# The fourth weight sum of a seven-product unit: an accumulating DMA from DRAM in the place of a VectorE instruction

## The chip, the cores and the metric

The kernel runs on one core of one Trainium2 chip. The metric is the device time of one execution in microseconds; three executions of the kernel before gave 2301.18, 2301.93 and 2302.52 us. TensorE, VectorE, ScalarE, GpSimd and SyncE are called PE, DVE, ACT, POOL and SP, as the profile calls them.

## The reference

Two decoder layers over 256 tokens of width 2048, all in float32. What concerns this change is the second half of a layer, the feed-forward part, and there only its matrix products with weights:

```python
h = rms_norm(x, ffn_norm[l])
x = x + (jax.nn.silu(h @ w_gate[l]) * (h @ w_up[l])) @ w_down[l]
```

`w_gate` and `w_up` are 2048 x 5632, `w_down` is 5632 x 2048, and the activations have 256 rows.

## The kernel before, in words

**Float32 by three products.** PE multiplies operands of a rounded float32 form. Each weight tile `raw` (128 partitions x 4 blocks x 512 columns, 1 MB) is split into two such tiles: ACT copies it to `wh`, which rounds it, and DVE subtracts, `wl = raw - wh`. The same is done to the activations, and `mm3` (line 836) issues three matmuls for each block: high x high, high x low, low x high. A product of four blocks is therefore twelve matmuls of 512 columns.

**Units.** In the feed-forward part the work is cut into units. A unit computes a 2 x 2 block of results (two halves of the tokens by two weight columns, for instance a block of `w_gate` and the same block of `w_up`) from a 2 x 2 block of weights. It uses a scheme with seven products in the place of eight, which needs sums of weight blocks and sums of activation blocks. The weight blocks are called b11, b12, b22 and b21. Sums are made in place by DVE with `w_sum`, one instruction for a whole tile. The activations' sums ("forms") are made once by `make_forms` and used by many units. A unit of `w_gate` and `w_up`, and most of `w_down`, has 4 blocks a product (`s` is 4); the last chunk's two `w_down` units of each layer have 2. There are 17 units in a layer, 34 in all. After its seven products a unit has plain products for the rest of its sum, which need no weight sums.

**The order of the seven.** The products run in the order p1, p5, p6, p2, p7, p3, p4. `early` makes e = b12 - b11 and b12 := b22 - b12 some items ahead. Then p1 splits b11 and makes b11 := b12 + b11; p5 splits e; p6 splits the new b11; p2 makes b11 := b21 - b11 (the sum that this change is about) and splits b21; p7 splits b12; p3 splits b22; p4 splits the last b11. The results are gathered in four PSUM banks, named C1, CX, CY and CZ in the trace (C, CX, CY, CZ where numbers are left out), so the products in this order write C, CZ, CX, C, CX, CY, CX: the fourth product, p2's, is the second run of C in a unit, and the seventh, p4's, is the CX run behind CY.

**What sets the order.** Every engine runs its instructions in the order in which the program lists them. A list of items is made; `prep` of an item (the splits and sums) is written out ahead of its `run` (the matmuls), as far ahead as six tile slots allow, which is three products of four blocks. A small model of the engines' queues (`Queues`, with costs in `act_cost` and `dve_cost`) decides at build time where other jobs (transposes, activation splits, residual sums) are written in between. All weight loads are issued by SP, line 796; a load waits until a slot among 22 is free.

Of the kernel before, what the change touches and what calls it, by code (L numbers as in the profile page):

```python
# [12 lines left out]
ALU = mybir.AluOpType  # L13
# [10 lines left out]
W = 512  # L24
# [8 lines left out]
KC = 4  # L33
HK = 2
S_GU = 4
FORMS = ("11", "22", "S1", "S3", "S2", "12", "S4")

SLOTS = 22
PLAIN_RAW, PLAIN_RING = 3, 4
# [102 lines left out]
def trunk_kernel(ctx: ExitStack, tc: tile.TileContext, aps: dict):  # L142
    nc = tc.nc
# [3 lines left out]
    dve = Engine(q, nc.vector, "dve", dve_cost)  # L147
# [16 lines left out]
    def slot(shape, dtype, name):  # L164

        return gen.tile(list(shape), dtype, tag="g", name=name)
# [55 lines left out]
    def add(steps, limit=BACKLOG_NS):  # L222
        jobs.append(Job(steps, limit))
        jobs.sort(key=lambda job: -job.limit)
# [7 lines left out]
    def drain(ready):  # L232
        stuck = 0
        while not ready():
            assert stuck < 2000, "operand is never made"
            stuck += 1
            q.pe += 100
            run_jobs(1000)
# [344 lines left out]
    class Forms:  # L583
# [5 lines left out]
        def at(self, f):  # L589
            h = self.halves[FORMS.index(f)]  # L590
            return h[:, 0, :self.s, :], h[:, 1, :self.s, :]
# [27 lines left out]
    def make_forms(F, xg):  # L619

        def quarter(t, h):
            return xg[:, h, :F.s, t * P:(t + 1) * P]
        a11, a12, a21, a22 = quarter(0, 0), quarter(0, 1), quarter(1, 0), quarter(1, 1)

        def split(f, src):
            hi, lo = F.at(f)
            act.activation(out=hi, in_=src, func=ACTF.Copy)
            dve.tensor_tensor(out=lo, in0=src, in1=hi.bitcast(F32), op=ALU.subtract)
            F.ready.add(f)
        split("11", a11)  # L630
        split("22", a22)
        dve.tensor_tensor(out=a22, in0=a21, in1=a22, op=ALU.add)
        dve.tensor_tensor(out=a21, in0=a11, in1=a21, op=ALU.subtract)
        yield
        split("S1", a22)
        split("12", a12)
        dve.tensor_tensor(out=a11, in0=a22, in1=a11, op=ALU.subtract)
        dve.tensor_tensor(out=a12, in0=a12, in1=a11, op=ALU.subtract)
        yield
        split("S2", a11)  # L640
        split("S3", a21)
        split("S4", a12)

# [50 lines left out]
    class Chunk:  # L694
# [32 lines left out]
        def form(self, f, k):  # L727
            drain(lambda: self.F is not None)
            return self.F.get(f, k)
# [61 lines left out]
    def dma_one(r):  # L791
        n = sum(src.shape[1] for src in r.srcs)
        r.tile = slot([P, n, W], F32, "raw")
        k = 0
        for src in r.srcs:
            nc.sync.dma_start(out=r.tile[:, k:k + src.shape[1], :], in_=src)
            k += src.shape[1]
        live[0] += 1
# [6 lines left out]
    def need(r):  # L805
        while r.tile is None:
            dma_one(raws[n_raw[0]])
            n_raw[0] += 1
        return r.tile

    def split_w(src, parts=1):

        n = src.shape[1]
        if 2 * n <= 4:
            both = slot([P, 2, n, W], F32R, "w")
            wh, wl = both[:, 0], both[:, 1]
        else:
            wh, wl = slot([P, n, W], F32R, "wh"), slot([P, n, W], F32R, "wl")
        saved, q.chain = q.chain, q.pe
        for k in range(parts):  # L820
            sl = slice(k * n // parts, (k + 1) * n // parts)
            act.activation(out=wh[:, sl, :], in_=src[:, sl, :], func=ACTF.Copy)
            dve.tensor_tensor(
                out=wl[:, sl, :], in0=src[:, sl, :], in1=wh[:, sl, :].bitcast(F32), op=ALU.subtract)
        q.chain = saved
        return wh, wl

    def w_sum(out, in0, in1, op):
        saved, q.chain = q.chain, q.pe
        dve.tensor_tensor(out=out, in0=in0, in1=in1, op=op)  # L830
        q.chain = saved

    def mm3(out, x, wh, wl, start, stop):
        hi, lo = x
        for n, (a, b) in enumerate(((hi, wh), (hi, wl), (lo, wh))):
            nc.tensor.matmul(  # L836
                out=out, lhsT=a, rhs=b, start=start and n == 0, stop=stop and n == 2,
                skip_group_check=True)
# [32 lines left out]
    def unit(s, quarter, plains, form, done, lead=1):  # L871

        bank = {}
        b11, b12, b22, b21 = (Raw([quarter(*kn)], UNIT_RAW) for kn in ((0, 0), (0, 1), (1, 1), (1, 0)))
        raws.extend((b11, b12, b22, b21))
        U = {}

        def new_bank(name):  # L880
            drain(lambda: mm_lease.free)
            mm_lease.free.pop(0)
            bank[name] = mm_p.tile([P, W], F32, tag="mm", name="C" + name)

        def copy(out, in_):
            saved, q.chain = q.chain, q.pe
            act.activation(out=out, in_=in_, func=ACTF.Copy)
            q.chain = saved

        def early():  # L890
            x11, x12, x22 = need(b11), need(b12), need(b22)
            U["e"] = slot([P, s, W], F32, "e")
            live[0] += 1
            w_sum(U["e"], x12, x11, ALU.subtract)
            w_sum(x12, x22, x12, ALU.subtract)

        def p1(it, parts=1):
            it.w = split_w(b11.tile)
            w_sum(b11.tile, b12.tile, b11.tile, ALU.add)

        def p5(it, parts=1):
            it.w = split_w(U["e"])
            live[0] -= 1

        def p6(it, parts=1):
            it.w = split_w(b11.tile)

        def p2(it, parts=1):
            w_sum(b11.tile, need(b21), b11.tile, ALU.subtract)
            it.w = split_w(b21.tile)  # L910
            live[0] -= 1

        def p7(it, parts=1):
            it.w = split_w(b12.tile)
            live[0] -= 1

        def p3(it, parts=1):
            it.w = split_w(b22.tile)
            live[0] -= 1

        def p4(it, parts=1):
            it.w = split_w(b11.tile)
            live[0] -= 1

        def product(it, f, name, start):
            wh, wl = it.w
            for k in range(s):
                x = form(f, k)
                mm3(bank[name], x, wh[:, k, :], wl[:, k, :], start and k == 0, k == s - 1)
                q.pe += 3 * MM_NS  # L930
                run_jobs()

        def r1(it):
            new_bank("1")
            product(it, "11", "1", True)
            new_bank("X")
            copy(bank["X"], bank["1"])

        def r5(it):
            new_bank("Z")  # L940
            product(it, "S1", "Z", True)
            U["s5"], U["s3"] = (tmp.tile([P, W], F32, tag="u", name=n) for n in ("s5", "s3"))
            copy(U["s5"], bank["Z"])

        def r6(it):
            product(it, "S2", "X", False)
            new_bank("Y")
            copy(bank["Y"], bank["X"])

        def r2(it):  # L950
            product(it, "12", "1", False)

        def r7(it):
            product(it, "S3", "X", False)
            copy(U["s3"], bank["X"])

        def r3(it):
            product(it, "S4", "Y", False)
            w_sum(bank["Z"], bank["Z"], U["s3"], ALU.add)

        def r4(it):
            product(it, "22", "X", False)
            w_sum(bank["Y"], bank["Y"], U["s5"], ALU.add)

        for p, r in ((p1, r1), (p5, r5), (p6, r6), (p2, r2), (p7, r7), (p3, r3), (p4, r4)):
            items.append(Item(1 if s <= 2 else 2, UNIT_RING, p, r))
        early_at[len(items) - 7 - lead] = early

        names = {(0, 0): "1", (1, 0): "Y", (0, 1): "X", (1, 1): "Z"}
        for i, (n, srcs, ops) in enumerate(plains):  # L970
            r = Raw(srcs, UNIT_RAW)
            raws.append(r)

            def prep(it, parts=1, r=r):
                it.w = split_w(need(r))
                live[0] -= 1

            def run(it, i=i, n=n, ops=ops):
                wh, wl = it.w
                for t in range(NT):  # L980
                    for k, op in enumerate(ops):
                        mm3(bank[names[n, t]], op(t), wh[:, k, :], wl[:, k, :], False, k == len(ops) - 1)
                        q.pe += 3 * MM_NS
                        run_jobs()
                    if i >= len(plains) - 2:
                        add(done(n, t, bank[names[n, t]]), FFN_LIMIT)
            items.append(Item(2, UNIT_RING, prep, run))
# [238 lines left out]
```

## Time and profile before

| | |
|---|---|
| three executions | 2301.18, 2301.93, 2302.52 us |
| median | 2301.93 us |
| the profiled execution | 2301.2 us |
| its span from the first to the last instruction | 2299.0 us |
| PE busy | 2261.3 us, 98% of the span |
| DVE busy | 1834.0 us, 80% |
| ACT busy | 1325.0 us, 58% |
| POOL busy | 52.4 us, 2% |
| granted clock of PE, mean | 0.999 of full speed |
| loads of weights | 438.69 MB on SP's queue, packets took 53.0% of 16 DMA engines' time |

The span is what the trace covers; 2.2 us of the execution's time lie around it. PE is busy nearly all of the time, so another engine matters only where PE stands and waits for it. The views that tell this are the groups of PE's instructions (their last columns give the idle time ahead of them and what ended it) and the timeline of one stretch, engine by engine.

### The profile page before, as it was taken

The page shows a single profiled execution, that of the slowest core. Times are in us where ns is not written, and L with a number is a line of the kernel's source. Part 1 is how long each engine was busy: PE and PEld are TensorE (multiplying, and loading weights), DVE is VectorE, ACT ScalarE, POOL GpSimd, SP SyncE. Part 2 cuts the span into 40 slices and gives each one's busy share as a digit, 9 for nine tenths or more (in the row PEclk, how much of TensorE's full clock was granted, in tenths as well). Part 3 has the DMA queues.
Part 4 walks back from the last instruction along what each step waited for, and adds up shares of the span by engine and source line. Part 5 has one row for each costly group of instructions (what it writes and reads, how often), then busy time and mean ns, then how long its engine had stood idle before and what let it go on. Part 6 is the DMA issues. An engine that isn't in the chain of part 4 may idle for free.

```text
span 2299.0 us, 25930 instructions
## 1 busy us (share of the span) xinstructions
PE 2261.3 (98%) x10249; PEld 1864.1 (81%) x10249; DVE 1834.0 (80%) x1721; ACT 1325.0 (58%) x1590; POOL 52.4 (2%) x36
## 2 busy tenths in 40 slices
PE   9999999999999999999999999999999999999999
PEld 7888888878788878888788888887787888788887
DVE  6666766889999898998765666768899998989986
ACT  6455565565664665656555555646656556556563
POOL 0100000000000000000000001000000000000000
PEclk9999999999999999999999999999999999999999
DMA  9554455454465644745545444554545556447453
GB/s 361 176 183 165 165 175 204 174 198 165 183 237 183 224 179 159 264 181 201 183 174 193 164 165 165 183 212 173 183 165 198 223 186 235 165 165 274 165 201 110
DMA packets 66937, 440.33 MB, mean 192 GB/s; under 512 B 8064, under 2 KB 8576, under 8 KB 16768
## 3 DMA queue, kind: packets, MB, share of 16 engines
q1 hardware_dynamic: 66816, 438.69, 53.0%
q8 instruction: 80, 1.31, 0.2%
q14 instruction: 41, 0.34, 0.0%
HBM read 436.56 MB, written 2.10 MB: 191 GB/s over the span
## 4 chain that ended last, share of the span: by engine, by line
PE 77%; DVE 13%; issue 5%; ACT 3%; DMA 2%; SPq 0%; DVEq 0%; ACTq 0%
PE Z L836 30%; PE CX L836 15%; PE C L836 12%; PE CY L836 9%; PE CZ L836 8%; DVE wl L90 6%; ACT wh L90 2%; DVE raw L90 1%; PE sc L462 1%; DVE w L90 1%; DVE e L90 1%; PE hTp L253 1%; DMA gn<-in_k_norm 1%; PE qkp L253 1%; DVE hF L90 1%
## 5 line engine op out<-in xcount | busy, mean ns | idle before, releaser
L90 DVE TENSOR_TENSOR wl<-raw,wh 128x2048 fp32r<-128x2048 f32 x316 | 717.3, 2287 | 139.3 <-ACT wh L90 136.5
L90 ACT ACTIVATE wh<-raw 128x2048 fp32r<-128x2048 f32 x316 | 597.0, 1912 | 165.3 <-PE CX L836 56.3
L836 PE MATMUL Z<-w,xT 128*128 128x512 f32 x2688 | 641.5, 395 | 1.8 <-DVE xT L90 1.0
L836 PEld LDWEIGHTS Z<-w,xT 128*128 128x128 f32 x2688 | 499.2, 188 | 106.2 <-DVE w L90 1.6
L90 DVE TENSOR_TENSOR w<-raw,w 128x1024 fp32r<-128x1024 f32 (+1 forms) x313 | 376.9, 1217 | 214.8 <-ACT w L90 209.7
L90 ACT ACTIVATE w<-raw 128x1024 fp32r<-128x1024 f32 (+1 forms) x313 | 315.5, 1049 | 28.2 <-DMA raw<-in_w_in 9.1
L90 DVE TENSOR_TENSOR raw<-raw 128x2048 f32<-128x2048 f32 (+1 forms) x102 | 220.7, 2164 | 2.5
L836 PE MATMUL CX<-wh,fF 128*128 128x512 f32 x528 | 175.5, 391 | 1.5 <-ACT s L90 1.5
L836 PE MATMUL C<-wh,fF 128*128 128x512 f32 x352 | 118.7, 393 | 0.0
L836 PEld LDWEIGHTS CX<-wh,fF 128*128 128x128 f32 x528 | 99.1, 188 | 23.5 <-ACT s L90 2.4
L836 PE MATMUL CY<-wh,fT 128*128 128x512 f32 x352 | 115.9, 390 | 0.4
L836 PE MATMUL C<-wh,fT 128*128 128x512 f32 x352 | 115.6, 389 | 0.0
L836 PE MATMUL CZ<-wh,fT 128*128 128x512 f32 x352 | 115.5, 389 | 0.0
L836 PE MATMUL CX<-wh,fT 128*128 128x512 f32 x352 | 115.5, 389 | 0.0
L836 PE MATMUL CX<-wl,fF 128*128 128x512 f32 x264 | 102.7, 389 | 0.0
L90 ACT ACTIVATE CX<-C 128x512 f32<-128x512 f32 x34 | 19.8, 582 | 125.0 <-PE C L836 125.0
L836 PE MATMUL Z<-w,bT 128*128 128x512 f32 x384 | 89.9, 391 | 0.0
L836 PE MATMUL Z<-w,aT 128*128 128x512 f32 x384 | 89.1, 390 | 0.0
L836 PEld LDWEIGHTS Z<-w,aT 128*128 128x128 f32 x384 | 71.8, 188 | 14.8
L836 PEld LDWEIGHTS Z<-w,bT 128*128 128x128 f32 x384 | 71.8, 188 | 14.7
L836 PE MATMUL CY<-wh,fF 128*128 128x512 f32 x240 | 78.9, 390 | 0.0
L836 PEld LDWEIGHTS CY<-wh,fT 128*128 128x128 f32 x352 | 66.1, 188 | 15.6 <-issue 2.0
(191 smaller groups left out, 3445.0 us busy)
## 6 DMA issues: line engine op xcount, KB each, us to landing
raw<-in_w_in SPq DMA_DIRECT2D x109, 1024.0 KB, 4.8
raw<-in_w_gate SPq DMA_DIRECT2D x88, 1024.0 KB, 4.8
raw<-in_w_up SPq DMA_DIRECT2D x88, 1024.0 KB, 4.9
raw<-in_w_down SPq DMA_DIRECT2D x72, 1024.0 KB, 4.9
raw<-in_w_out SPq DMA_DIRECT2D x32, 1024.0 KB, 4.8
raw<-in_w_down SPq DMA_DIRECT2D x32, 512.0 KB, 4.6
raw<-in_w_in SPq DMA_DIRECT2D x5, 512.0 KB, 8.1
xstage<-in_xT SPq DMA_DIRECT2D x8, 256.0 KB, 7.4
```

The lines of the kernel that those rows point to most:

```text
L90: return f(**kw)
L253: nc.tensor.transpose(out=tp[:, i, t * P:(t + 1) * P], in_=src_of(t)[:, (c0 + i) * P:(c0 + i + 1) * P], identity=ident)
L462: nc.tensor.matmul(out=sc[:, g, :n], lhsT=L.kv[pair, g][:, h, t * P:(t + 1) * P], rhs=kT[:, h, :n], start=True, stop=True)
L836: nc.tensor.matmul(out=out, lhsT=a, rhs=b, start=start and n == 0, stop=stop and n == 2, skip_group_check=True)
```

## The change

The sum of p2 is no longer made by DVE. Behind the split of p6, POOL issues a DMA that reads b21's weights from DRAM a second time and adds them to what stands in b11's tile. Since a DMA adds and doesn't subtract here, the tile must hold the negative of the old sum by then, so p1 makes b11 := e - b22 in the place of b12 + b11, and the form S2 of the activations becomes its negative. Every DMA moves one tile; `max_dma_last_dim` cuts it into pieces of 256 elements, 1 KB, so that a tile of 1 MB has 1024 pieces where a plain load's rows are 8 KB long.

```diff
-FORMS = ("11", "22", "S1", "S3", "S2", "12", "S4")
+FORMS = ("11", "22", "S1", "S3", "-S2", "12", "S4")
...
-        dve.tensor_tensor(out=a11, in0=a22, in1=a11, op=ALU.subtract)
-        dve.tensor_tensor(out=a12, in0=a12, in1=a11, op=ALU.subtract)
+        dve.tensor_tensor(out=a11, in0=a11, in1=a22, op=ALU.subtract)
+        dve.tensor_tensor(out=a12, in0=a12, in1=a11, op=ALU.add)
         yield
-        split("S2", a11)
+        split("-S2", a11)
...
         def p1(it, parts=1):
             it.w = split_w(b11.tile)
-            w_sum(b11.tile, b12.tile, b11.tile, ALU.add)
+            w_sum(b11.tile, U["e"], b22.tile, ALU.subtract)
...
         def p6(it, parts=1):
             it.w = split_w(b11.tile)
+            nc.gpsimd.dma_start(
+                out=b11.tile, in_=quarter(1, 0), accum_op=ALU.add, max_dma_last_dim=2 * W)
 
         def p2(it, parts=1):
-            w_sum(b11.tile, need(b21), b11.tile, ALU.subtract)
-            it.w = split_w(b21.tile)
+            it.w = split_w(need(b21))
             live[0] -= 1
...
         def r6(it):
-            product(it, "S2", "X", False)
+            product(it, "-S2", "X", False)
```

In DVE's queue, in the fourth unit of the first layer (the one whose products begin at 574.8 us in the trace), stood before the splits of p5 to p4 and the sum, where `raw_4184` is b11, `raw_4252` b21, `raw_4204` b12, `raw_4224` b22 and `e_4282` is e:

```order
L90 TENSOR_TENSOR raw_4184<-raw_4204,raw_4184 128x2048
L90 TENSOR_TENSOR wl_4347<-e_4282,wh_4346 128x2048
...
L90 TENSOR_TENSOR wl_4386<-raw_4184,wh_4385 128x2048
L90 SCALAR_TENSOR_TENSOR s_4361<-CZ_4116,r20_3634,s_4361 128x512
L90 TENSOR_TENSOR raw_4184<-raw_4252,raw_4184 128x2048
L90 TENSOR_TENSOR wl_4407<-raw_4252,wh_4406 128x2048
L90 TENSOR_TENSOR wl_4429<-raw_4204,wh_4428 128x2048
L90 TENSOR_TENSOR wl_4449<-raw_4224,wh_4448 128x2048
L90 TENSOR_TENSOR wl_4467<-raw_4184,wh_4466 128x2048
```

and in the same place of the changed kernel stands:

```order
L90 TENSOR_TENSOR raw_4184<-e_4282,raw_4224 128x2048
L90 TENSOR_TENSOR wl_4347<-e_4282,wh_4346 128x2048
...
L90 TENSOR_TENSOR wl_4386<-raw_4184,wh_4385 128x2048
L90 SCALAR_TENSOR_TENSOR s_4361<-CZ_4116,r20_3634,s_4361 128x512
L90 TENSOR_TENSOR wl_4407<-raw_4252,wh_4406 128x2048
L90 TENSOR_TENSOR wl_4429<-raw_4204,wh_4428 128x2048
L90 TENSOR_TENSOR wl_4449<-raw_4224,wh_4448 128x2048
L90 TENSOR_TENSOR wl_4467<-raw_4184,wh_4466 128x2048
```

The second sum into `raw_4184` is gone, and the splits of p2, p7, p3 and p4 follow the split of p6 directly; the first sum has other operands and the same place.

In ACT's queue of the changed kernel, in the same unit from the copy ahead of p6 on, the order is that of before, and the semaphores that each instruction waits for are named behind it:

```order
L90 ACTIVATE s5_4425<-CZ_4412 128x512 [waits PE_49]
L90 ACTIVATE wh_4428<-raw_4204 128x2048 [waits DVE_49]
L90 ACTIVATE CY_4446<-CX_4404 128x512 [waits DVE_49,PE_49]
L90 ACTIVATE wh_4448<-raw_4224 128x2048 [waits DMAHW4_49,DVE_49]
L90 ACTIVATE wh_4466<-raw_4184 128x2048 [waits DMASW3_49,DVE_49]
L90 ACTIVATE s3_4426<-CX_4404 128x512 [waits PE_49]
L90 ACTIVATE wh_4485<-raw_4350 128x2048 [waits DMAHW6_49,DVE_49]
L90 ACTIVATE wh_4504<-raw_4410 128x2048 [waits DMAHW7_49,DVE_49]
```

The copy of p4 (`wh_4466`) waits in addition for DMASW3, the semaphore of POOL's DMA; the copy of CX for p7's result and the copies of the plain products stand behind it in the queue.

In POOL's queue of the changed kernel, at the start of the first layer's feed-forward part, stand:

```order
L90 TENSOR_TENSOR ra_3048<-rsq,mhalf 128x2
L907 DMA raw<-in_w_gate 128x8x256
L90 TENSOR_TENSOR r_3634<-rsq,mhalf 128x2
L907 DMA raw<-in_w_gate 128x8x256 x3
L907 DMA raw<-in_w_down 128x8x256 x2
L907 DMA raw<-in_w_gate 128x8x256 x4
```

Before, only the two small instructions stood there; one DMA a unit is new, 17 in a layer, and little else stands between them.

## Rows read from the trace of the kernel before

**Rows 1.** The page: busy times with their shares, and SP's DMA queue.

```profile
PE 2261.3 (98%) x10249; PEld 1864.1 (81%) x10249; DVE 1834.0 (80%) x1721; ACT 1325.0 (58%) x1590; POOL 52.4 (2%) x36
...
q1 hardware_dynamic: 66816, 438.69, 53.0%
```

**Rows 2.** PE's groups by shape: busy us, mean ns of one | idle ahead, releaser.

```profile
L836 PE MATMUL C<-wl,fF 128*128 128x512 f32 x176 | 69.0, 392 | 4.9 <-DVE wl L90 4.9
...
L836 PE MATMUL C<-wl,hF 128*128 128x512 f32 x64 | 25.9, 404 | 6.0 <-DVE wl L90 6.0
```

**Rows 3.** Timeline of DVE, unit at 662 us: start, us, instruction, [idle ahead <-releaser].

```profile
664.38 2.29 DVE L90 TENSOR_TENSOR wl<-raw,wh 128x2048 fp32r<-128x2048 f32 x1 [0.79 <-ACT wh L90]
...
667.19 2.28 DVE L90 TENSOR_TENSOR raw<-raw 128x2048 f32<-128x2048 f32 x1
669.39 6.88 DVE L90 TENSOR_TENSOR wl<-raw,wh 128x2048 fp32r<-128x2048 f32 x3
676.51 2.29 DVE L90 TENSOR_TENSOR wl<-raw,wh 128x2048 fp32r<-128x2048 f32 x1 [0.24 <-ACT wh L90]
```

**Rows 4.** Timeline of PE in the same unit.

```profile
670.45 0.39 PE L836 MATMUL C<-wh,hF 128*128 128x512 f32 x1
671.73 0.50 PE L836 MATMUL C<-wl,hF 128*128 128x512 f32 x1 [0.90 <-DVE wl L90]
...
679.80 0.39 PE L836 MATMUL CX<-wh,hF 128*128 128x512 f32 x1
680.02 0.39 PE L836 MATMUL CX<-wl,hF 128*128 128x512 f32 x1
```

**Rows 5.** Timeline of ACT, unit at 662 us.

```profile
674.56 1.92 ACT L90 ACTIVATE wh<-raw 128x2048 fp32r<-128x2048 f32 x1 [0.93 <-PE C L836]
```

**Rows 6.** Timelines of DVE, ACT and PE, unit at 575 us.

```profile
578.80 2.28 DVE L90 TENSOR_TENSOR wl<-raw,wh 128x2048 fp32r<-128x2048 f32 x1
...
583.86 8.89 DVE L90 TENSOR_TENSOR wl<-raw,wh 128x2048 fp32r<-128x2048 f32 x4
...
588.38 1.92 ACT L90 ACTIVATE wh<-raw 128x2048 fp32r<-128x2048 f32 x1 [1.21 <-DVE wl L90]
...
586.20 0.50 PE L836 MATMUL C<-wl,fF 128*128 128x512 f32 x1 [1.24 <-DVE wl L90]
...
594.50 0.39 PE L836 MATMUL CX<-wl,fF 128*128 128x512 f32 x1
```

**Rows 7.** Timelines of DVE, ACT and PE, unit at 620 us.

```profile
621.38 2.29 DVE L90 TENSOR_TENSOR wl<-raw,wh 128x2048 fp32r<-128x2048 f32 x1 [1.32 <-ACT wh L90]
...
633.37 2.29 DVE L90 TENSOR_TENSOR wl<-raw,wh 128x2048 fp32r<-128x2048 f32 x1 [0.23 <-ACT wh L90]
...
631.41 1.92 ACT L90 ACTIVATE wh<-raw 128x2048 fp32r<-128x2048 f32 x1 [1.00 <-PE C L836]
...
628.79 0.50 PE L836 MATMUL C<-wl,hF 128*128 128x512 f32 x1 [0.60 <-DVE wl L90]
...
638.03 0.39 PE L836 MATMUL CX<-wl,hF 128*128 128x512 f32 x1
```

**Rows 8.** Timelines of DVE, ACT and PE, unit at 745 us.

```profile
743.23 2.28 DVE L90 TENSOR_TENSOR wl<-raw,wh 128x2048 fp32r<-128x2048 f32 x1
...
755.87 4.50 DVE L90 TENSOR_TENSOR wl<-raw,wh 128x2048 fp32r<-128x2048 f32 x2 [0.43 <-ACT wh L90]
...
753.93 3.71 ACT L90 ACTIVATE wh<-raw 128x2048 fp32r<-128x2048 f32 x2
...
762.52 0.39 PE L836 MATMUL CX<-wl,fF 128*128 128x512 f32 x1
```

**Rows 9.** DMA issues: count, KB each, median us from issue to landing.

```profile
raw<-in_w_gate SPq DMA_DIRECT2D x88, 1024.0 KB, 4.8
```

**Rows 10.** SP's queue in the unit at 662 us (the span of three issues).

```profile
667.69 6.96 SPq L796 DMA_DIRECT2D raw<-in_w_down  x3
```

**Rows 11.** POOL's groups by shape.

```profile
L90 POOL TENSOR_TENSOR qf<-rsq,mhalf 128x8 f32<-128x8 f32 x16 | 35.6, 2227 | 375.9 <-DVE rsq L90 375.9
```

## The prediction

> **What bounds the kernel now.** I read the page first: PE is busy 98% of the span, DVE 80% [rows 1]. The reader should see that work taken from DVE is worth nothing by itself; it pays only where PE stands and DVE is what ends the wait. So I went to the groups of PE's instructions with their idle time. In the feed-forward part, two groups carry nearly all of what DVE's splits cost: the low halves into bank C, 4.9 us and 6.0 us, ended by `wl` [rows 2]. C's low half is what the product of p2 (and of p1) waits for.
>
> The timeline of one such unit shows why. DVE ends p6's split at 664.38 + 2.29 = 666.67 us, makes the sum into b11 from 667.19 on for 2.28 us, and only then, at 669.39, the split of p2 [rows 3]. PE has begun the product of p2 at 670.45 and stands 0.90 us until that split is there [rows 4]. The sum stands ahead of the split for which PE waits, and it isn't needed itself until p4. The same stop is 1.24 us long in the unit at 575 us and 0.60 us in the one at 620 us [rows 6, 7]. Four stops of 1.24 us make the 4.9, four pairs of 0.60 and 0.90 the 6.0 [rows 2]: twelve units of 34 have this stop. The other units of four blocks look like the one at 745 us, where DVE itself waits for ACT [rows 8].
>
> **What the change removes.** 34 DVE sums, 30 of them of 2.28 us as in [rows 3], the four of two-block units half as large: some 73 us of DVE. At most the twelve stops come back. A stop costs PE its idle time and a pipeline that refills: matmuls start 679.80 and 680.02, so 0.22 us apart, and each lasts 0.39 [rows 4], hence 0.17 us more. That is 1.41, 1.07 and 0.77 us, four of each: 13.0 us. DVE's split of p2 would come 2.2 us sooner, more than any of the stops, so they go entirely. The rest of the 73 us only lengthens DVE's own idle time.
>
> The changed sum of p1 reads two tiles and writes one as before and keeps its place; e and b22 are both there when `early` has run on the same engine. I price it at nothing, and the forms' changed signs too: same instructions, same sizes. If p1's sum were later by some tenths, the split of e behind it would be the one to show it.
>
> **What it adds, and when that has to be done.** Each unit gets a DMA that may start when p6's split is made and must have landed before ACT copies b11 for p4. Behind that copy in ACT's queue stand the copy of CX and the splits of the plain products, so PE then runs out of everything. The time that a unit allows is read off the timelines in three steps: from the end of p6's split to the start of ACT's copy for p4; plus how much earlier than needed p4's split ends; less the stop that vanishes, since PE then comes sooner.
>
> - Unit at 662 us: 666.67 to 674.56 is 7.9 us [rows 3, 5]; p4's split ends at 676.51 + 2.29 = 678.80, the matmul that needs it starts at 680.02 [rows 3, 4], 1.2 us; less 1.07: 8.0 us.
> - Unit at 575 us: 581.08 to 588.38 is 7.3; the four splits end at 592.75, needed at 594.50, 1.75; less 1.41: 7.6 us [rows 6].
> - Unit at 620 us: 623.67 to 631.41 is 7.7; 635.66 against 638.03, 2.4; less 0.77: 9.3 us [rows 7].
> - Unit at 745 us: p6's split ends at 745.51, ACT's second copy begins half way through its pair, near 755.7: 10.2; 760.37 against 762.52, 2.15; no stop: 12.4 us [rows 8].
>
> So the twelve units that can gain are the ones that allow least. I take 12.4 us for all 18 others of four blocks, and leave out the four two-block units, which move half a tile.
>
> **How long the DMA takes.** No DMA of the trace adds, and none is issued by POOL; I bound it by the loads. The queue moved 438.69 MB, 418 tiles of 1 MB, and its packets took 53.0% of 2299 us [rows 1]: 2.9 us a tile on all 16 engines. Issue to landing is 4.8 us [rows 9], so 1.9 us lie outside the transfer. Bound below: it goes like a lone load, 4.8 us. But to add in place, a DMA has to fetch the old sum as well as the new weights, twice the bytes of a load: 5.8 us. And it isn't alone: SP issues loads at 667.69 and twice more within 7 us [rows 10]. One that meets it and shares the engines adds 2.9 us, two add 5.8. So L, from p6's split to landing, is 1.9 + 5.8 + 2.9 = 10.6 us with one, 13.5 us with two. I take 13, near the upper, since two issues fall into the first 4 to 5 us of each stretch. Pieces of 1 KB and POOL's part are priced at nothing here; were they like POOL's own slowest small instruction, 2.2 us [rows 11], that comes on top.
>
> The Trainium skill (Collectives: The Full Stack, Part 3, on the bandwidth ceiling) says that a reduction by the DMA engines issues two reads for each piece on the same read ring and so runs at half of a copy's rate, 62.28 against 32.35 GB/s. No run here shows it. By it the transfer is 5.8 us, not 2.9; with one read and one equal share of a load the sum would be L = 7.7 and 2289 us.
>
> **The sum**, against the profiled execution's own 2301.2 us (the median of the three is 0.7 us higher, inside their spread). With positive differences only:
>
> time = 2301.2 - 13.0 + 4 x [(L - 7.6) + (L - 8.0) + (L - 9.3)] + 18 x (L - 12.4).
>
> For L = 13: 4 x (5.4 + 5.0 + 3.7) = 56.4, and 18 x 0.6 = 10.8; 2301.2 - 13.0 + 67.2 = 2355 us, 2.4% slower.
>
> **The rivals.**
>
> *It lands in time (faster).* With one read's cost, or loads that stay out of its way, L is 4.8 to 7.7 us and the stops vanish for nothing: 2288 to 2289 us. It decides at L = 8.8 (two kinds of unit late by 1.2 and 0.8 us, 2296 us). For it: engines are busy only 53% of the time. Against: the loads come in just these stretches, since the product phase frees slots. Chance 0.17.
>
> *It comes out even.* Between L = 8.8 and 9.7 the stops given back and the new ones cancel: 2297 to 2305 us. A change below 0.2%, 4.6 us, can't be told from none here. Chance 0.08.
>
> *POOL is late as well (much slower).* If writing out a thousand pieces waits for DVE, each DMA is later by up to one DVE instruction, 2.3 us [rows 3], or by POOL's own 2.2 [rows 11]: L = 15.3, and 4 x 21.0 + 18 x 2.9 = 136, so 2424 us; with both loads met in full, L = 15.8 and 2439 us. For it: in all of these stretches DVE runs one two-operand instruction behind the other. Chance of L above 15: 0.15.
>
> The Trainium skill (SBUF — State Buffer, who interferes with whom) states that POOL cannot write descriptors while DVE is in a two-port mode, and that an instruction with two tensor operands has no such mode. By that this rival's first half falls away. No row here has a DMA of POOL's.
>
> *Loads come late instead.* A unit's eight loads take 23 us of the engines in the 42 us from one unit to the next (620 to 662); 5.8 more make 29. Only a load that ACT waits for costs something, and slots run far enough ahead that I price this at nothing beyond L.
>
> **How the numbers follow.** Likeliest, 0.60: L between 9.7 and 15, 2305 to 2415 us, at 13 us 2355. The range takes in the landing in time below (2288) and POOL's lateness with both loads above (2440); beyond it is left what a still slower DMA would give, about 1 in 10. Faster 0.17, same 0.08, slower 0.60 + 0.15 = 0.75.
>
> **What the profile after would show.** Right: the `raw<-raw` sums of DVE fewer by 34; no idle time ahead of C's low halves in the twelve units; idle ACT ahead of `wh<-raw` ended by a DMA of POOL's, 12 units by some 4 to 5 us; PE idle ahead of the last CX of a unit; POOL's issues landing after 11 to 15 us. Wrong: landings under 9 us and no wait of ACT for them, or stops ahead of C that stay though the sum is gone, which would mean that ACT's copy and not DVE set them. Wrong in size: landings beyond 15 us, or ones that differ much from unit to unit.

## The result, and the profile after

| | before | after |
|---|---|---|
| median, lowest to highest | 2302.22 us, 2301.18 to 2306.3 | 2643.64 us, 2632.2 to 2654.5 (4 executions) |
| ratio, 95% interval | | 1.1479, 1.1428 to 1.1529 |
| profiled execution, span | 2301.2, 2299.0 us | 2654.5, 2652.8 us |
| PE busy | 2261.3 us | 2345.3 us |
| granted clock of PE, mean | 0.999 | 0.936 |

The changed kernel is 15% slower; the prediction was 2355 us and its range ended at 2440. The page after, its busy times, the granted clock in 40 slices (tenths) and the queues (q0 is POOL's):

```profile
PE 2345.3 (88%) x10249; PEld 1916.3 (72%) x10249; DVE 1769.6 (67%) x1687; ACT 1323.9 (50%) x1590; POOL 103.7 (4%) x70
...
PEclk9999999998989988899999999998989899888999
...
q1 hardware_dynamic: 66816, 438.69, 45.6%
q0 software_dynamic: 33312, 33.56, 8.0%
```

Against [rows 1]: DVE does 34 instructions and 64 us less, as the change says, and PE, which has the same 10249 matmuls, is busy 84.0 us longer and stands 307.5 us in the place of 37.7. In the slices of the two feed-forward parts PE's clock is no longer full. Who waits for whom is told by the waits (us in total, times, longest):

```profile
DVE wl L90 <- ACT wh L90: 525.7, 176, 20.7
PE CX L836 <- ACT s L90: 249.9, 31, 17.8
ACT wh L90 <- DMA raw<-in_w_gate: 238.0, 22, 16.8
ACT wh L90 <- DMA raw<-in_w_down: 99.1, 7, 21.0
PE CX L836 <- DVE wl L90: 23.3, 28, 1.0
PE CX L836 <- ACT CY L90: 17.0, 3, 8.9
...
ACT w L90 <- DMA raw<-in_w_down: 18.4, 4, 8.6
```

ACT waits for a DMA in 29 of the 30 units of four blocks, and in the four two-block ones too (the last row); PE then waits 31 times, 3 of them as before, for what stands behind that in ACT's queue. The stops ahead of C's low halves [rows 2] are gone. And this is how long the DMAs take from issue to landing (median), and the loads, 4.8 us before [rows 9]:

```profile
raw<-in_w_gate SPq DMA_DIRECT2D x88, 1024.0 KB, 5.9
raw<-in_w_up SPq DMA_DIRECT2D x88, 1024.0 KB, 7.4
...
raw<-in_w_gate POOLq DMA_DIRECT2D x22, 1024.0 KB, 19.6
...
raw<-in_w_down POOLq DMA_DIRECT2D x8, 1024.0 KB, 19.3
```

One of the longest stops, in ACT's, PE's, SP's and POOL's timelines:

```profile
712.85 1.91 ACT L90 ACTIVATE wh<-raw 128x2048 fp32r<-128x2048 f32 x1
735.81 1.91 ACT L90 ACTIVATE wh<-raw 128x2048 fp32r<-128x2048 f32 x1 [21.05 <-DMA raw<-in_w_down]
737.62 0.58 ACT L90 ACTIVATE s<-CX 128x512 f32<-128x512 f32 x1
...
738.25 0.80 PE L836 MATMUL CX<-wh,hF 128*128 128x512 f32 x1 [17.77 <-ACT s L90]
740.10 0.79 PE L836 MATMUL CX<-wl,hF 128*128 128x512 f32 x1 [1.05 <-DVE wl L90]
...
709.40 5.77 SPq L796 DMA_DIRECT2D raw<-in_w_down  x3
717.12 0.33 SPq L796 DMA_DIRECT2D raw<-in_w_gate  x1
717.79 3.05 SPq L796 DMA_DIRECT2D raw<-in_w_up  x2
...
708.67 1.54 POOL L907 DMA_DIRECT2D raw<-in_w_down  x1 [48.05 <-DVE wl L90]
```

POOL issues at 708.67, behind p6's split, as foreseen. While its DMA is in flight SP issues six loads, and ACT gets b11 at 735.8. The row that names `s` as PE's releaser hides the cause one step: `s<-CX` is the copy of p7's result, which stands behind p4's `wh` in ACT's queue. This DMA's landing, and the queues (packets, MB, share of 16 engines) in two windows of its flight, 714 to 715 us, where its first pieces go, and 720 to 725 us:

```profile
raw<-in_w_down POOLq DMA_DIRECT2D x1, 1024.0 KB, 27.0
...
q0 software_dynamic: 152, 0.16, 98.4%
q1 hardware_dynamic: 18, 0.03, 10.6%
...
q1 hardware_dynamic: 213, 1.61, 79.9%
q0 software_dynamic: 216, 0.22, 27.3%
```

With SP's queue nearly empty POOL's takes the engines alone, 152 pieces in 1 us. With loads there the two queues complete equally many packets, 213 and 216 in 5 us (in the next unit 522 and 524 from 774 to 786 us), but SP's carry 1.61 MB and POOL's 0.22; at that pace 1024 pieces take 24 us. (The shares add up to 107%: packets of the two queues overlap a little in time.) What the stop does to PE behind it shows in windows of 2 us (start and end, length, PE busy and matmuls, weight loads, DVE, ACT, POOL, then granted clock, DMA share, GB/s):

```profile
740.00:742.00 2.00, 1.90 (x5) 1.52 (x6) 2.00 (x2) 1.91 (x2) 0.00 (x0) 0.50 0.00 0
742.00:744.00 2.00, 2.00 (x6) 1.60 (x5) 2.00 (x3) 0.00 (x0) 0.00 (x0) 0.52 0.00 0
744.00:746.00 2.00, 2.00 (x10) 1.64 (x9) 1.74 (x2) 1.55 (x1) 0.00 (x0) 1.00 0.24 33
```

After 17.8 us without work PE goes on at 0.50 of full speed, the lower of its two levels, 1.2 GHz, and does 5 to 6 matmuls in 2 us where it does 10 at 2.4 GHz.

**Where the time went**, from these rows: the three waits ahead of CX, 249.9 + 23.3 + 17.0 us, less the 5.8 that they had before (rows below), are 284.4; the stops of C give back 10.9 [rows 2]; PE is busy 84.0 us longer. That is 357.5 us; the spans differ by 353.8.

```profile
PE CX L836 <- ACT s L90: 4.0, 3, 2.5
...
PE CX L836 <- ACT CY L90: 1.8, 3, 1.1
```

### The profile page after: what moved, and what is told of

Its sections match the earlier page's. It is cut to its first block, busy times and chain, and to the rows that moved or that the text cites. A ratio compares the mean times of both kernels' runs of the same rounds, so it can differ in the third digit from the quotient of the medians.

```text
span 2652.8 us, 26056 instructions
## 1 busy us (share of the span) xinstructions
PE 2345.3 (88%) x10249; PEld 1916.3 (72%) x10249; DVE 1769.6 (67%) x1687; ACT 1323.9 (50%) x1590; POOL 103.7 (4%) x70
## 3 DMA queue, kind: packets, MB, share of 16 engines
q1 hardware_dynamic: 66816, 438.69, 45.6%
q0 software_dynamic: 33312, 33.56, 8.0%
## 5 line engine op out<-in xcount | busy, mean ns | idle before, releaser
L836 PE MATMUL CX<-wh,fF 128*128 128x512 f32 x528 | 207.8, 456 | 168.5 <-ACT s L90 168.5
L90 ACT ACTIVATE w<-raw 128x1024 fp32r<-128x1024 f32 (+1 forms) x313 | 315.5, 1049 | 45.2 <-DMA raw<-in_w_down 18.4
L836 PEld LDWEIGHTS CX<-wh,fF 128*128 128x128 f32 x528 | 118.2, 224 | 203.0 <-ACT s L90 177.8
L836 PE MATMUL CX<-wh,hF 128*128 128x512 f32 x192 | 76.5, 464 | 77.9 <-ACT s L90 77.9
L836 PE MATMUL CX<-wl,fF 128*128 128x512 f32 x264 | 121.7, 461 | 16.3 <-DVE wl L90 16.3
L836 PEld LDWEIGHTS CX<-wh,hF 128*128 128x128 f32 x192 | 43.9, 229 | 90.7 <-ACT s L90 81.3
L836 PEld LDWEIGHTS CX<-wl,fF 128*128 128x128 f32 x264 | 58.8, 223 | 37.6 <-DVE wl L90 25.6
L90 DVE TENSOR_TENSOR wl<-e,wh 128x2048 fp32r<-128x2048 f32 x30 | 68.6, 2288 | 21.2 <-ACT wh L90 21.1
## 6 DMA issues: line engine op xcount, KB each, us to landing
raw<-in_w_gate POOLq DMA_DIRECT2D x22, 1024.0 KB, 19.6
```

What stands on the lines that cost most here:

```text
L90: return f(**kw)
L836: nc.tensor.matmul(out=out, lhsT=a, rhs=b, start=start and n == 0, stop=stop and n == 2, skip_group_check=True)
```

## The experiments

The theory formed from the result: the engines serve the two queues in turn, packet by packet, so that 1 KB pieces get an eighth of what 8 KB rows get, loads that come later overtake the adding DMA, and ACT's queue waits. Rivals: adding itself is slow; POOL is slow to write the pieces; loads held up by POOL's traffic cost the time; the signs or the order do. Edits are to the changed kernel unless said otherwise; "landing" is the median of the 22 `in_w_gate` DMAs of POOL.

### No addition: copy_1k

```diff
-                out=b11.tile, in_=quarter(1, 0), accum_op=ALU.add, max_dma_last_dim=2 * W)
+                out=b11.tile, in_=quarter(1, 0), max_dma_last_dim=2 * W)
```

> The DMA of each unit copies b21 over b11 in the same 1 KB pieces and adds nothing, so p4 multiplies with b21 in the place of the sum. Theory of turns (while loads are in flight, each DMA engine takes one packet of SP's queue, 8 KB, then one of POOL's, 1 KB): it still lands late, median 13 to 18 us, because the pieces are as many; time 2390 to 2480 us. Rival, adding itself is slow: without it the DMA goes like a load of small pieces, lands in 6 to 8 us, and the time falls to 2288 to 2300 us. Rival, POOL writes the pieces out late: landing and time stay near 19.6 us and 2640 us.

2315.89 us, ratio 1.006 (1.004 to 1.008), landing 9.2 us. This lies between the theory of turns and the rival that adding is slow, outside the ranges of both. The page says why it isn't the test it was meant to be:

```profile
q0 software_dynamic: 8736, 33.56, 4.3%
```

Without the addition the same 33.56 MB went in 8736 packets and not in 33312: the plain copy's 1 KB pieces travelled as packets of 4 KB, so that the number of turns fell too. What it does show is the price of adding alone: 4.3% of a span of 2316.5 us for 32 MB is 3.1 us a tile, and 5.6 to 6.6 us where the DMA adds (below). The run to set beside it is add_4k below, which adds in the same 8736 packets: there the landing is 12.9 us and the time 2409.2, so at this size adding itself costs 3.7 us of landing and 93 us of time. That rival is a part of the loss, and not all of it.

### Pieces of 8 KB: add_8k

```diff
-                out=b11.tile, in_=quarter(1, 0), accum_op=ALU.add, max_dma_last_dim=2 * W)
+                out=b11.tile, in_=quarter(1, 0), accum_op=ALU.add)
```

> The same adding DMA with whole rows of 8 KB as pieces. Theory of turns: one piece for one load packet, 8 turns on each engine in the place of 64; landing 10 to 12 us, time 2310 to 2350 us. Rival, adding itself is slow: the bytes are the same, so landing stays near 19 us and the time near 2640 us. Rival, POOL's writing out: an eighth of the pieces, so landing falls to 10 us or less and the time to 2290 to 2320 us; copy_1k tells this one from the turns.

2348.9 us, ratio 1.0207 (1.019 to 1.0224). The page, the landing, and the queues in 5 us (586 to 591) in which both have work:

```profile
q0 software_dynamic: 4896, 33.56, 7.7%
...
raw<-in_w_gate POOLq DMA_DIRECT2D x22, 1024.0 KB, 11.0
...
q0 software_dynamic: 85, 0.70, 68.1%
q1 hardware_dynamic: 86, 0.70, 35.0%
```

Landing and time are what the theory of turns expected. Same addition, same engine time (7.7% of 2345.8 us is 5.6 us a tile, against 6.6 with 1 KB), but equal packets are now equal bytes, 0.70 MB each, and the landing comes 8.6 us sooner. Some 295 of the 341 us that the change costs go with the size of the pieces.

### Loads in 1 KB pieces too: loads_1k

```diff
-            nc.sync.dma_start(out=r.tile[:, k:k + src.shape[1], :], in_=src)
+            nc.sync.dma_start(out=r.tile[:, k:k + src.shape[1], :], in_=src, max_dma_last_dim=2 * W)
```

> The adding DMA as in the change, but SP's loads of line 796 cut into 1 KB pieces too. Theory of turns: a turn of the loads is then some 0.05 us long and not 0.3, so the adding DMA lands in 11 to 13 us although there are more packets in all; time 2320 to 2380 us. Rivals, adding is slow or POOL is late: nothing is gained, landing stays near 19 us; the loads, with eight times the packets, take some half a microsecond more each, and the time is 2640 us or above.

2410.41 us, ratio 1.0471 (1.045 to 1.0491); landing 12.6 us as expected, the time above. POOL's DMA is that of the change, untouched, and lands 7 us sooner with SP's packets small as well. In 4 us (739 to 743) in which both queues have work:

```profile
q0 software_dynamic: 465, 0.48, 73.4%
q1 hardware_dynamic: 466, 0.48, 43.7%
```

This separates turns from POOL's own slowness: POOL issues the same 1024 pieces in the same 1.5 us. The time is that of 4 KB pieces (next), whose landing is the same within 0.3 us.

### Pieces of 4 KB: add_4k

```diff
-                out=b11.tile, in_=quarter(1, 0), accum_op=ALU.add, max_dma_last_dim=2 * W)
+                out=b11.tile, in_=quarter(1, 0), accum_op=ALU.add, max_dma_last_dim=8 * W)
```

> The changed kernel with pieces of 4 KB. If packets are served in turn, half the bytes of a load's row per turn give a landing between those of 8 KB (11.0 us) and 1 KB (19.6 us), nearer to the former, 12 to 14.5 us for gate, and 2365 to 2410 us. Rival: the size of a piece matters only through the engines' time for it (102 ns for 1 KB, 629 ns for 8 KB, so 6.5 against 5.0 us a tile): the landing is within 0.7 us of that of 8 KB, and the time 2345 to 2358 us.

2409.2 us, ratio 1.0465 (1.045 to 1.0481), landing 12.9 us; the engines' time for a tile is that of 8 KB (7.5% of 2408.1 us, 5.6 us). Between the two, and at the upper edge of what turns gave; the rival, engine time alone, fails by 50 us. (Its 629 ns and 5.0 us a tile for 8 KB pieces were too low: 7.7% of add_8k's span is 5.6 us a tile.)

### The sum left out: no_sum

```diff
-            nc.gpsimd.dma_start(
-                out=b11.tile, in_=quarter(1, 0), accum_op=ALU.add, max_dma_last_dim=2 * W)
```

> Neither the DMA nor the fourth sum: p4 multiplies with what p1 left in b11. This is the most that taking the sum from DVE can give. By the prediction's term for the twelve stops: 2301.2 - 13.0 = 2288 to 2290 us, and no idle time ahead of C's low halves in hF. Rival, ACT's copies and not DVE set those stops: 2300 to 2302 us.

2285.75 us, ratio 0.9933 (0.9918 to 0.9947): 16 us below before, and 2 below what was expected. C's low halves wait no more, and matmuls there take 389 ns for 392 and 404:

```profile
L836 PE MATMUL C<-wl,fF 128*128 128x512 f32 x176 | 68.5, 389 | 0.0
...
L836 PE MATMUL C<-wl,hF 128*128 128x512 f32 x64 | 24.9, 389 | 0.0
```

### The signs alone: signs

The kernel before with the change's signs and DVE's fourth sum kept; of its edits to the kernel before, the two in the weights' sums:

```diff
-            w_sum(b11.tile, b12.tile, b11.tile, ALU.add)
+            w_sum(b11.tile, U["e"], b22.tile, ALU.subtract)
...
-            w_sum(b11.tile, need(b21), b11.tile, ALU.subtract)
+            w_sum(b11.tile, need(b21), b11.tile, ALU.add)
```

> The changed signs alone: p1 makes e - b22, the form is -S2, and DVE adds b21 in p2 where it stood before; no DMA. Prediction's term: nothing, 2300 to 2304 us. Rival, the sum of p1 is later or slower for waiting on e: 2306 us or more.

2301.61 us, ratio 1.000 (0.9991 to 1.0009). The signs cost nothing.

### DVE's sum moved: sum_in_p7

The kernel before, with the sum behind p7's split in the place of ahead of p2's.

```diff
         def p2(it, parts=1):
-            w_sum(b11.tile, need(b21), b11.tile, ALU.subtract)
-            it.w = split_w(b21.tile)
+            it.w = split_w(need(b21))
...
         def p7(it, parts=1):
             it.w = split_w(b12.tile)
+            w_sum(b11.tile, b21.tile, b11.tile, ALU.subtract)
```

> The kernel before, with DVE's fourth sum moved behind the split of p7; no DMA. Theory (the stop in p2 comes from the sum standing ahead of p2's split): the stops ahead of C's low halves go. If DVE has no room later, they come back at p3 or p4, and the time stays within 2298 to 2304 us; if it has room, 2289 to 2293 us. I expect the former, since p7's and p4's splits were early by only 0.7 and 1.2 us in the unit at 662 us.

2304.41 us, ratio 1.0012 (1.0003 to 1.0021), at the edge of what was expected. The stops ahead of C's low halves are gone, but among PE's waits stands a new one, of the same size as the 10.9 us that vanished:

```profile
PE CY L836 <- DVE wl L90: 11.4, 13, 1.0
```

The product of p3 waits for DVE instead. So the sum gains nothing by this place; what gains is that DVE doesn't spend the 2.3 us among these splits at all. A place behind p3's split was not tried.

### The DMA's result unread: add_unread

```diff
         def p4(it, parts=1):
-            it.w = split_w(b11.tile)
+            it.w = split_w(b22.tile)
```

> The change's DMA, 1 KB pieces, but p4 splits b22 a second time in the place of b11, so nothing on an engine reads what the DMA adds; the slot of b11 is still held until it has landed. Theory of p4's wait: the stops ahead of the last CX go, and what stays is what the loads lose to the DMA and to the held slot, 2330 to 2450 us. Rival, the loads' lateness is the whole loss: 2600 us or more. If late loads cost nothing: 2286 to 2295 us.

2479.93 us, ratio 1.0774 (1.0754 to 1.0793), above the range of p4's wait and below that of the rival. The experiment wasn't clean: once p4 doesn't read it, b11's slot goes on to another tile, and ACT and SP's queue wait for DMAs by up to 16.6 us, longer than a load takes to land (6.1 us here), which fits a wait of that tile for the landing.

```profile
ACT wh L90 <- DMA raw<-in_w_gate: 117.8, 10, 16.6
...
SPq L796 <- DMA raw<-in_w_gate: 101.7, 10, 10.6
```

It left open whether the loads' delay costs by itself; the next two runs test that.

### The DMA into a tile of its own: no_aside and add_aside

The control is `no_sum` with 21 slots and one instruction of one element on DVE; the second adds the change's DMA behind it:

```diff
-SLOTS = 22
+SLOTS = 21
...
+    side_w = const.tile([P, D], F32, name="side_w")
+    nc.gpsimd.memset(side_w, 0.0)
...
         def p6(it, parts=1):
             it.w = split_w(b11.tile)
+            dve.tensor_scalar(out=side_w[:, :1], in0=side_w[:, :1], scalar1=0.0, scalar2=0.0,
+                              op0=ALU.mult, op1=ALU.add)
+            nc.gpsimd.dma_start(
+                out=side_w.rearrange("p (s w) -> p s w", w=W)[:, :s, :], in_=quarter(1, 0),
+                accum_op=ALU.add, max_dma_last_dim=2 * W)
```

> Control for the next: no DMA of POOL's, DVE's fourth sum left out (so p4's product is not the reference's), 21 tile slots in the place of 22, and one instruction of one element a unit on DVE behind p6's split, on a tile of its own. If slots run ahead far enough, as the prediction took it, the time is that of the kernel without the sum at 22 slots, 2285.8 us, within 5: 2283 to 2292 us. Rival: the loads are short of slots already, and it is 2300 us or more.

> The control with the change's DMA issued in the same place, 1 KB pieces, adding into the tile of its own, for whose landing nothing waits but the next unit's instruction of one element (p4's product isn't the reference's). If the loss of the change is the wait for the landing, and the slow clock behind that wait, this is at most 25 us above its control, the loads' landing being longer (7 us for 4.9), with few stops of PE. Rival: the loads held up by POOL's queue, or the traffic itself, cost as much: 60 us or more above the control, with ACT or SP's queue waiting for loads.

The control runs at 2302.93 us (2302.31 to 2307.15), not at 2283 to 2292: the slot less and the small instruction cost 17 us together, as the rival of few slots had it (PE stands 40.1 us, 25.9 in `no_sum`); which of the two does it is open. With the DMA it is 2302.84 us (2301.8 to 2306.55); both stand at 1.001 of before, 0.9999 to 1.002. The DMAs are about as slow as in the change, and loads come later than the control's 4.8 us:

```profile
raw<-in_w_gate SPq DMA_DIRECT2D x88, 1024.0 KB, 7.4
...
side_w<-in_w_gate POOLq DMA_DIRECT2D x22, 1024.0 KB, 16.3
...
side_w<-in_w_down POOLq DMA_DIRECT2D x8, 1024.0 KB, 24.6
```

So 34 landings, with medians of 12 to 25 us by kind, loads late by 2.6 us and the traffic cost nothing that can be measured, as long as nobody waits for the landing; PE stands 38.3 us, no more than in the control. This was shown in a kernel that is 17 us slower than `no_sum` for another reason. The loss is the wait, and the clock that falls with it.

### p4 later: late_add_8k, late_add_1k, late_before

p4 is put behind the first two plain products of its unit, which have 24 matmuls each (two halves of the tokens), and so give the DMA more time (the 10.9 us of the first expectation; the 5 to 6 us of the second are too few): in the kernel with 8 KB pieces, in the changed kernel with its 1 KB, and in the kernel before, with DVE's sum and no DMA.

```diff
-        for p, r in ((p1, r1), (p5, r5), (p6, r6), (p2, r2), (p7, r7), (p3, r3), (p4, r4)):
+        for p, r in ((p1, r1), (p5, r5), (p6, r6), (p2, r2), (p7, r7), (p3, r3)):
...
-        early_at[len(items) - 7 - lead] = early
+        early_at[len(items) - 6 - lead] = early
...
+            if i == 1:
+                items.append(Item(1 if s <= 2 else 2, UNIT_RING, p4, r4))
```

> The adding DMA with 8 KB pieces, and p4 (split and product) put behind the first two plain products of its unit. Theory (the loss is p4's wait for the landing, and its size is landing less what the unit allows): two plain products are 48 matmuls of 0.227 us, 10.9 us more to land in; with landings of 11 to 12 us no unit waits, the twelve stops are gone, and the time is near that without a sum: 2284 to 2295 us, no idle ACT ended by POOL's DMA. Rival, the DMA slows the loads and holds b11's slot, and this costs whether or not p4 waits: 2305 to 2350 us, with ACT waiting for SP's loads.

> The changed kernel with its 1 KB pieces, p4 behind the first two plain products. If engines serve POOL's queue and SP's in turn, packet by packet, the landing stays at 17 to 20 us, the two products (some 5 to 6 us) don't cover it, and the time is 2390 to 2470 us with stops ahead of the last CX in fewer units. Rival: the place of p4 alone decided and the size of the pieces matters little, 2285 to 2300 us.

> The kernel before with p4 put behind the first two plain products of its unit; DVE's sum stays and there is no POOL DMA. If the gain of the late order with 8 KB pieces (2291.3 us) comes from the sum that DVE no longer makes, the twelve stops ahead of C's low halves stay here (some 13 us in all) and the time is 2299 to 2316 us. Rival: the order alone is what gained, and this kernel runs at 2286 to 2295 us without those stops or with them.

| | median us | ratio, 95% interval | landing us |
|---|---|---|---|
| 8 KB pieces, late p4 | 2291.28 | 0.9955 (0.9941 to 0.9968) | 11.6 |
| 1 KB pieces, late p4 | 2440.39 | 1.061 (1.0593 to 1.0628) | 21.9 |
| before, late p4 | 2319.51 | 1.0081 (1.0066 to 1.0096) | none |

The first beats both kernels: 10 us below before, 352 below the change. Its page and ACT's only waits for POOL's DMA:

```profile
PE 2258.4 (99%) x10249; PEld 1864.3 (81%) x10249; DVE 1765.6 (77%) x1687; ACT 1324.1 (58%) x1590; POOL 82.0 (4%) x70
...
ACT wh L90 <- DMA raw<-in_w_down: 3.2, 4, 1.6
...
ACT wh L90 <- DMA raw<-in_w_gate: 1.5, 2, 1.1
```

It takes both: with 1 KB pieces the two products aren't enough (the time is as expected, the landing 2 us above). Nor is the order the gain; by itself it costs 18 us, 3.5 above the range expected. The stops ahead of C's low halves stay, and DVE holds up PE in another place too:

```profile
PE C L836 <- DVE wl L90: 12.7, 12, 1.2
PE CY L836 <- DVE CY L90: 9.8, 12, 1.2
```

PE stands 11.2 us longer than in the kernel before and is busy 6.3 us longer, at a mean granted clock of 0.996. The new stop isn't the sum's doing: without DVE's sum, with 8 KB pieces, 7.4 of its 9.8 us are still there. In this order the change with 8 KB pieces is worth 28 us, 2319.5 against 2291.3; of the 26.9 us between the profiled spans the C stops are 12.7, the rest of PE's idle time 5.0 and its busy time 9.2.

## Why the prediction was wrong

**Right.** What the change removes: the stops ahead of C's low halves go entirely, and without the DMA the kernel gains 16 us where 13.0 was worked out; the signs are worth nothing; DVE does 34 instructions less. Right, too, were the direction and the mechanism of the wait: ACT's copy for p4 waits for POOL's landing, and PE stands ahead of the last CX of a unit. The prediction's own sign of a wrong size, landings beyond 15 us, came true. That loads come late was priced at nothing, and add_aside bears that out, though they land 2.6 us later.

**The price of the transfer** was nearly right: 5.8 us of all engines for an adding tile was assumed, twice a load's 2.9; it took 6.6 in 1 KB pieces and 5.6 in larger ones, and 3.1 as a plain copy. The Trainium skill (Collectives: The Full Stack, Part 3) says that a reduction by the DMA engines runs at half of a copy's rate because it reads two sources; this kernel agrees to that extent, 5.6 against 3.1 us, a factor of 1.8, at the same 8736 packets.

**The step that failed** is "One that meets it and shares the engines adds 2.9 us, two add 5.8 ... I take 13". The landing is 19.6 us. Sharing was taken as equal time, which would have let the DMA get away after two loads. In the chip's rows the queues share by packets. A packet of SP's took 290 ns and carried 6.6 KB on average (45.6% of 16 engines' 2652.8 us, and 438.69 MB, over 66816), one of POOL's 102 ns and 1.0 KB (8.0%, 33.56 MB, 33312). While loads are there, 64 pieces on each of 16 engines take 64 x (290 + 102) ns = 25 us and not 6.6, and every load that SP issues meanwhile gets in between. In the unit above six did: 1.9 + 6.6 + 6 x 2.9 = 25.9 us by the prediction's own formula, against 27.0 measured. That it comes so near is partly luck: by the packets 5.33 MB of loads, five tiles, went by from 714.0 to 735.4 us, and POOL's first pieces started 5.3 us behind the issue. So the formula holds roughly, and the number of loads that meet the DMA was wrong, because it depends on how slow the DMA is made. The Trainium skill (DMA: Bandwidth & Descriptors, Queues, rings and completion order) says that an engine goes round its queues one packet at a time; 213 against 216 packets in 5 us agree. The prediction didn't weigh that rule, and priced the size of the pieces at nothing: that was the choice which cost most.

**The sum's other terms.** From the measured landings the formula gives the waits, from the rows come those ahead of CX (the three kinds above, less 5.8) and PE's longer busy time:

| pieces | landing us | waits by the formula | waits measured | PE busier by | of it by the clock | mean granted clock |
|---|---|---|---|---|---|---|
| 8 KB | 11.0 | 4 x (3.4 + 3.0 + 1.7) = 32 | 37 | 21 us | 17 us | 0.991 |
| 4 KB | 12.9 | 4 x (5.3 + 4.9 + 3.6) + 18 x 0.5 = 64 | 78 | 40 us | 34 us | 0.978 |
| 1 KB | 19.6 | 4 x (12.0 + 11.6 + 10.3) + 18 x 7.2 = 265 | 284 | 84 us | 80 us | 0.936 |

So the waits by the units' allowances of 7.6 to 12.4 us were good to some 20%, and 2553 us would have been the forecast with the right landing. The two-block units, which the prediction left out, add 18.4 us to ACT's waits. Of the 101 us to the profiled execution's 2654.5, most is a term that the sum didn't have at all: PE's matmuls go on at half the clock behind a long stop. In the trace's clock records PE is busy for 164 us at half the clock, for 3 us before; the same matmuls take half as long at the full clock (0.39 us against 0.80), so 80 of the 84.0 us are the clock.

**The rivals.** "POOL is late as well" named the right side but not the cause: POOL's issue takes 1.5 us for 1024 adding pieces and 0.86 for 128 rows, too little for it. "It lands in time" took 8 KB pieces and the later p4 here, and then gives 2291 us, near that rival's 2288 to 2289.

## What to carry to other kernels

A DMA that somebody waits for, issued beside another queue's traffic, should have packets as large as that traffic's: the wait is set by bytes per turn, and everything that the other queue issues meanwhile counts, so that a slow transfer meets more and becomes slower. Before work is moved from a busy engine to a DMA, find the first instruction that reads its result and move that back by the landing measured under load; the same slow DMA costs nothing where nothing waits for it. And price a long stop of PE above its idle time, for the clock falls with it: here 284 us of waits brought 80 us more, while the stops of about 1 us before left the mean granted clock at 0.999.

## What the runs showed of the hardware that was not expected

- While both queues have work, they complete equal numbers of packets on the 16 engines, whatever their sizes: 213 of SP's and 216 of POOL's in 5 us (7.6 and 1.0 KB), 86 and 85 in 5 us (both 8.2 KB), 466 and 465 in 4 us (both 1.0 KB).
- An adding DMA keeps its pieces as packets (33312 for 33.56 MB in pieces of 1 KB), while a plain copy with the same limit of 1 KB went in 8736, as an adding one with a limit of 4 KB.
- Adding costs the engines 5.6 to 6.6 us of packet time for 1 MB, a copy 3.1 us.
- After a stop of 17.8 us PE ran its next 6 us at the 1.2 GHz level; over the kernel PE was busy 84 us longer with the same matmuls.
